# Separate tiles for the sums of weight blocks, and one place fewer for the partner blocks, in a Strassen gate and up projection

## The chip, the cores and the metric

One Trainium2 chip (trn2), one of its cores. The metric is the device time of one launch in microseconds; a kernel's time is the median of its runs. Engines are named as the profile names them: PE (TensorE's matmuls), PEld (its weight loads), DVE (VectorE), ACT (ScalarE), POOL (GpSimd) and SP (the queue that issues most transfers).

## The reference, cut to what matters

One layer of a decoder is computed for 1024 prompt rows and 32 sample rows: a mixer of convolution and attention, then a feed-forward part, then a last norm. The change lies in the feed-forward part alone:

```python
h2 = _rmsnorm(x, norm2_g) * (1 + sc2) + sh2
ffn = (jax.nn.silu(h2 @ w_gate) * (h2 @ w_up)) @ w_down
x = x + ga2 * ffn
```

All of it is in float32, with 1024 features, 2816 hidden features and 1056 rows.

## The kernel before, in words

Activations lie transposed: features on the 128 partitions, rows along the free dimension. A float32 product is made of three matmuls in a reduced format: the operand is split into a high part (`wh`, `xh`: a rounded copy by ACT) and a low part (`wl`, `xl`: operand minus high part, by DVE), and high x high, high x low and low x high are summed in PSUM.

The 1056 rows are cut into two **lanes** of 528, and each lane into halves of 264. For gate and for up, `block_product` (line 1357) makes, by a Strassen scheme of seven block products instead of eight, two blocks of 128 output columns at once: block f and its partner f + 11. `combos` (line 1234) makes the seven split operands of a lane; `weight_units` (line 1318) yields the seven split weight operands. A call of `block_product` is called a **product** here: seven **steps** (the loop at line 1389), each of four k-blocks with three matmuls per lane (lines 1396 to 1398). There are 24 products: gate and up of f = 0 for lane 0 alone, while lane 1 is still being normalised (line 1444); gate and up of f = 1 to 10 for both lanes; and between f = 4 and 5 the two of f = 0 for lane 1 (line 1451). Steps add into three PSUM banks; in between a partial product is held by ACT (`hold`, line 1379), and results go to the tile sg by DVE (`put`, line 1363). POOL then stores sg in a_d (line 1435).

For each product `weight_units` loads two raw tiles on the SP queue: r1 with the 1024 x 128 weights of block f (line 125, in the pool wp, tag raw, three places, which the high part of w_out's tiles used before and the loads of activations for the down projection use after, line 1487) and r2 with those of its partner f + 11 (line 1323, in a pool of its own, w3, three places). With a11 and a12 the halves of r1 and a21 and a22 those of r2, the weight operands of the seven steps are a11, a12, s2, s1, s3, s4, a22, where

```python
s1 = a21 + a22   (line 1340, tile sw)      s3 = a11 - a21   (line 1341, over a21)
s2 = s1 - a11    (line 1342, over a11)     s4 = a12 - s2    (line 1343, over a12)
```

POOL makes the four sums, 128 x 512 elements each. Four splits are made per product: r1 as a whole (ACT at line 131, DVE at line 137, 1024 columns), then the pairs (s2, s1) and (s3, s4), then a22 (ACT at line 1332, which the profile counts under line 93, and DVE at line 1333, 512 columns each). Their tiles wh and wl have two places each, so a split can be made when the one two before it has been used up.

Since s2 and s4 are written over r1, they wait until DVE has split r1, and r1's place is free only when s2 and s4 have been split. r2's place is free when s3 and a22 have been.

The order of the instructions on each engine is not written out here: it is set when the program is built, by priority and by what is ready. The weight loads, sums and splits are traced at high priority. After each product up to two of the 24 copies of the caches, DRAM to DRAM, are put on the SP queue behind the last r2 load (line 1426).

Ahead of this stage stands the output projection (`out_product`, line 1183) with the squares and sums for norm2 (`norm2_square`, line 1202); norm2 of the second lane and its `combos` run on ACT and DVE beside the first two products (lines 1439 to 1445). Behind it comes the down projection: `load_a` (line 1481) loads activations from a_d into the places of r1 and splits them (lines 1491 and 1492), and `load_down` (line 1496) loads and splits w_down.

Of the kernel before, what the change touches and what calls it, by code (L numbers as in the profile page):

```python
# [10 lines left out]
F32 = mybir.dt.float32  # L11
# [7 lines left out]
P = 128  # L19
D = 1024  # L20
KT = 8
# [38 lines left out]
def hybrid_step(  # L60
# [9 lines left out]
    nc = tc.nc  # L70
# [13 lines left out]
    def nm(s):  # L84
        cnt[0] += 1
        return f"{s}_{cnt[0]}"
# [5 lines left out]
    def act(out, in_, func=AF.Copy, **kw):  # L92
        return nc.scalar.activation(out, in_, func, **kw)  # L93
# [28 lines left out]
    def load_raw(src, nk):  # L122
        raw = wp.tile([P, T], F32, tag="raw", bufs=3, name=nm("raw"))[:, :D].rearrange("p (k c) -> p k c", c=P)
        with in_order(last_w[1]):
            last_w[0] = nc.sync.dma_start(raw[:, :nk], src)
        return raw
# [7 lines left out]
    def split_raw(raw, nk):  # L134
        wh, wl = split_high(raw, nk)
        with in_order(pre_done[0]):
            nc.vector.tensor_sub(wl[:, :nk], raw[:, :nk], wh[:, :nk].bitcast(F32))  # L137
        return wh, wl
# [1144 lines left out]
    sw = tc.alloc_tile_pool(name="sw", bufs=1, side="right", reuse_waits="tile")  # L1283
# [14 lines left out]
    w3 = tc.alloc_tile_pool(name="w3", bufs=1, reuse_waits="tile")  # L1298
# [19 lines left out]
    def weight_units(w, f):  # L1318

        with tc.high_priority():  # L1320
            r1 = load_raw(w[:, :, P * f:P * f + P], KT)
            r2 = w3.tile([P, KT, P], F32, tag="raw", bufs=3, name=nm("raw"))
            last_w[0] = nc.sync.dma_start(r2, w[:, :, P * (f + FH):P * (f + FH) + P])
            s1 = sw.tile([P, 4, P], F32, tag="sw", bufs=2, name=nm("sw"))

        def pair(p, q):
            wh = wp.tile([P, KT, P], F32R, tag="wh", bufs=2, name=nm("wh"))
            wl = wp.tile([P, KT, P], F32R, tag="wl", bufs=2, name=nm("wl"))
            for i, x in enumerate((p, q)):
                if x is not None:  # L1330
                    h = wh[:, 4 * i:4 * i + 4]
                    act(h, x)
                    nc.vector.tensor_sub(wl[:, 4 * i:4 * i + 4], x, h.bitcast(F32))  # L1333
            return [(wh, wl, 0), (wh, wl, 4)]


        a11, a12, a21, a22 = r1[:, 0:4], r1[:, 4:8], r2[:, 0:4], r2[:, 4:8]
        with tc.high_priority():
            u = split_raw(r1, KT)
            nc.gpsimd.tensor_add(s1, a21, a22)  # L1340
            nc.gpsimd.tensor_sub(a21, a11, a21)
            nc.gpsimd.tensor_sub(a11, s1, a11)
            nc.gpsimd.tensor_sub(a12, a12, a11)
        s2, s3, s4 = a11, a21, a12
        yield (*u, 0)
        yield (*u, 4)
        with tc.high_priority():
            u = pair(s2, s1)
        yield from u
        with tc.high_priority():  # L1350
            u = pair(s3, s4)
        yield from u
        with tc.high_priority():
            u = pair(a22, None)
        yield u[0]

    def block_product(w, f, lanes, sgs, up, hook=None):

        units = weight_units(w, f)
        banks = [[ps("s") for _ in lanes], [ps("pt") for _ in lanes], [ps("mm") for _ in lanes]]  # L1360
        keep = {}
# [232 lines left out]
```

## Time and profile before

| | before |
|---|---|
| time, median of 3 runs | 1378.84 us (1377.95 to 1380.05) |
| the profiled execution's own time | 1376.94 us |
| its span, first to last instruction | 1375.2 us |
| mean granted clock of TensorE | 0.966 of full speed |
| PE busy | 1307.9 us, 95% of the span |
| PEld busy | 1206.0 us, 88% |
| DVE busy | 716.9 us, 52% |
| ACT busy | 499.6 us, 36% |
| POOL busy | 212.1 us, 15% |

All rows come from one profiled execution; times are counted from its first instruction. In a row of the timeline stand the start, the duration, the engine, the line of the kernel, the operation, what is written from what, the shapes and the count, and in brackets how long the engine had been idle and what ended that. A row of the waits names the engine and what it was about to do, and behind the arrow who released it; then the total, the number of times and the longest. In a row of the chain stand start, duration and the work that the end of the program was waiting for. PE is counted as busy from a matmul's start to its modelled end. A wait for several things is put down to the last of them.

### The profile page before, as it was taken

What the parts mean: (1) busy time and instruction counts of PE and PEld (TensorE: products, weight loads), DVE (VectorE), ACT (ScalarE), POOL (GpSimd) and SP (SyncE); (2) the same over time, 40 slices, a digit from 0 to 9 for tenths busy, and PEclk for the clock granted to TensorE, in tenths of its full rate; (3) what the DMA queues carried; (4) which work ended last, traced back from release to release, by engine and by line L of the source; (5) the groups of instructions that cost most, each with busy time, mean ns of one, the idle gap of its engine ahead of it and who ended that gap; (6) DMA issues with size and microseconds to landing.
All of it is one profiled execution on the core that took longest, in us unless ns stands there. A gap on an engine that the chain in (4) does not pass through costs nothing.

```text
span 1375.2 us, 23628 instructions
## 1 busy us (share of the span) xinstructions
PE 1307.9 (95%) x9488; PEld 1206.0 (88%) x9488; DVE 716.9 (52%) x1448; ACT 499.6 (36%) x1077; POOL 212.1 (15%) x235
## 2 busy tenths in 40 slices
PE   8999998999899999996999999999999599999996
PEld 7767686859588979995999999999999599999996
DVE  5732364137324968779554465554454435353465
ACT  5442515242423325636333344333344302020244
POOL 3700000000000001232323233332231000000000
PEclk9999999969899999998999999999999899999998
DMA  9957474337463965783436344332451534141343
GB/s 315 310 194 256 147 256 151 93 101 255 123 182 103 236 217 168 245 261 109 143 120 231 100 184 132 108 109 83 162 188 61 197 132 141 47 141 47 95 152 128
DMA packets 188093, 220.80 MB, mean 161 GB/s; under 512 B 12426, under 2 KB 159367, under 8 KB 187472
## 3 DMA queue, kind: packets, MB, share of 16 engines
q1 hardware_dynamic: 169550, 173.89, 39.5%
q0 software_dynamic: 11504, 41.96, 9.1%
q10 hardware_dynamic: 6930, 3.45, 1.0%
q8 instruction: 74, 1.21, 0.4%
q14 instruction: 35, 0.29, 0.1%
HBM read 182.11 MB, written 64.21 MB: 179 GB/s over the span
## 4 chain that ended last, share of the span: by engine, by line
PE 73%; DVE 9%; issue 8%; DMA 7%; POOL 2%; ACT 1%; SPq 1%; DVEq 0%; POOLq 0%; ACTq 0%
PE pss L1398 6%; PE pss L1397 6%; PE pss L1396 6%; PE psmm L162 4%; PE psmm L163 4%; PE psmm L164 4%; PE pss L1509 3%; PE pss L1510 3%; PE pss L1511 3%; PE psmm L1509 3%; PE psmm L1510 3%; PE psmm L1511 3%; PE psmm L1397 3%; PE psmm L1396 3%; PE psmm L1398 3%
## 5 line engine op out<-in xcount | busy, mean ns | idle before, releaser
L93 ACT ACTIVATE wh<-raw 128x512 fp32r<-128x512 f32 (+2 forms) x200 | 152.7, 775 | 440.4 <-PE psmm L163 91.2
L1396 PE MATMUL pss<-xh,wh 128*128 128x264 f32 x704 | 201.1, 286 | 12.8 <-ACT wh L93 9.6
L1398 PE MATMUL pss<-xh,wl 128*128 128x264 f32 x704 | 201.2, 286 | 3.7 <-DVE wl L1333 3.4
L1397 PE MATMUL pss<-xl,wh 128*128 128x264 f32 x704 | 200.8, 285 | 0.0
L162 PE MATMUL psmm<-hh,wh 128*128 128x384 f32 (+1 forms) x528 | 176.9, 335 | 0.0
L163 PE MATMUL psmm<-hl,wh 128*128 128x384 f32 (+1 forms) x528 | 175.8, 333 | 0.0
L164 PE MATMUL psmm<-hh,wl 128*128 128x384 f32 (+1 forms) x528 | 174.7, 331 | 0.0
L137 DVE TENSOR_TENSOR wl<-raw,wh 128x1024 fp32r<-128x1024 f32 (+2 forms) x103 | 107.3, 1043 | 97.8 <-ACT wh L93 54.1
L1333 DVE TENSOR_TENSOR wl<-raw,wh 128x512 fp32r<-128x512 f32 x96 | 89.2, 940 | 118.3 <-ACT wh L93 117.0
L1396 PEld LDWEIGHTS pss<-xh,wh 128*128 128x128 f32 x704 | 133.4, 190 | 13.7 <-ACT wh L93 9.8
L1398 PEld LDWEIGHTS pss<-xh,wl 128*128 128x128 f32 x704 | 132.9, 189 | 5.0 <-DVE wl L1333 4.4
L1397 PEld LDWEIGHTS pss<-xl,wh 128*128 128x128 f32 x704 | 133.4, 189 | 0.0
L162 PEld LDWEIGHTS psmm<-hh,wh 128*128 128x128 f32 x528 | 100.8, 191 | 14.7 <-issue 11.5
L163 PEld LDWEIGHTS psmm<-hl,wh 128*128 128x128 f32 x528 | 100.9, 191 | 5.3 <-issue 4.9
L164 PEld LDWEIGHTS psmm<-hh,wl 128*128 128x128 f32 x528 | 101.4, 192 | 3.1 <-issue 2.8
L1396 PE MATMUL psmm<-xh,wh 128*128 128x264 f32 x352 | 101.0, 287 | 0.3 <-ACT wh L93 0.2
L1397 PE MATMUL psmm<-xl,wh 128*128 128x264 f32 x352 | 100.6, 286 | 0.0
L1398 PE MATMUL psmm<-xh,wl 128*128 128x264 f32 x352 | 100.1, 285 | 0.0
L1509 PE MATMUL pss<-ah,wh 128*128 128x384 f32 (+1 forms) x264 | 86.2, 326 | 14.7 <-ACT wh L93 14.7
L1510 PE MATMUL pss<-al,wh 128*128 128x384 f32 (+1 forms) x264 | 85.8, 325 | 0.0
L1511 PE MATMUL pss<-ah,wl 128*128 128x384 f32 (+1 forms) x264 | 85.7, 325 | 0.0
L1509 PE MATMUL psmm<-ah,wh 128*128 128x384 f32 (+1 forms) x264 | 85.4, 324 | 0.0
(324 smaller groups left out, 2896.8 us busy)
## 6 DMA issues: line engine op xcount, KB each, us to landing
ring<-in_w_ada_dram SPq DMA_DIRECT2D x32, 512.0 KB
out_dram<-in_cache_kv_dram SPq DMA_DIRECT2D x8, 2040.0 KB
raw<-in_w_in_dram SPq DMA_DIRECT2D x24, 512.0 KB
raw<-in_w_gate_dram SPq DMA_DIRECT2D x24, 512.0 KB
raw<-in_w_up_dram SPq DMA_DIRECT2D x24, 512.0 KB
a_d<-sg POOLq DMA_DIRECT2D x22, 528.0 KB, 3.3
a<-a_d SPq DMA_DIRECT2D x22, 528.0 KB
raw<-in_w_down_dram SPq DMA_DIRECT2D x48, 192.0 KB
```

The source lines that it names most:

```text
L93: return nc.scalar.activation(out, in_, func, **kw)
L137: nc.vector.tensor_sub(wl[:, :nk], raw[:, :nk], wh[:, :nk].bitcast(F32))
L162: nc.tensor.matmul(out, wh[:, k], h, start=(i == 0), stop=False)
L163: nc.tensor.matmul(out, wh[:, k], l, start=False, stop=False)
L164: last = nc.tensor.matmul(out, wl[:, k], h, start=False, stop=(i == n - 1))
L1333: nc.vector.tensor_sub(wl[:, 4 * i:4 * i + 4], x, h.bitcast(F32))
L1396: nc.tensor.matmul(o, wh[:, k0 + k], hi[:, k], start=st, stop=False, skip_group_check=True)
L1397: nc.tensor.matmul(o, wh[:, k0 + k], lo[:, k], start=False, stop=False, skip_group_check=True)
L1398: last = nc.tensor.matmul(o, wl[:, k0 + k], hi[:, k], start=False, stop=(k == 3), skip_group_check=True)
L1509: nc.tensor.matmul(o[:, :n], wh, ah[:, t0:t0 + n], start=(j == 0), stop=False)
L1510: nc.tensor.matmul(o[:, :n], wh, al[:, t0:t0 + n], start=False, stop=False)
L1511: nc.tensor.matmul(o[:, :n], wl, ah[:, t0:t0 + n], start=False, stop=(j == 2 * nf - 1))
```

## The change

s1, s2 and s4 get tiles of their own, from the pool sw, whose tag sw has four places instead of two; s3 is still written over a21. The pool w3, for r2, has two places instead of three. The order of the four sums in the text becomes s1, s2, s3, s4. Per partition the pool sw grows by 4 KB and w3 shrinks by 4 KB. Loads, splits, matmuls and the number of sums are the same.

```diff
         with tc.high_priority():
             r1 = load_raw(w[:, :, P * f:P * f + P], KT)
-            r2 = w3.tile([P, KT, P], F32, tag="raw", bufs=3, name=nm("raw"))
+            r2 = w3.tile([P, KT, P], F32, tag="raw", bufs=2, name=nm("raw"))
             last_w[0] = nc.sync.dma_start(r2, w[:, :, P * (f + FH):P * (f + FH) + P])
-            s1 = sw.tile([P, 4, P], F32, tag="sw", bufs=2, name=nm("sw"))
+            s1, s2, s4 = [sw.tile([P, 4, P], F32, tag="sw", bufs=4, name=nm("sw")) for _ in range(3)]
...
             u = split_raw(r1, KT)
             nc.gpsimd.tensor_add(s1, a21, a22)
+            nc.gpsimd.tensor_sub(s2, s1, a11)
             nc.gpsimd.tensor_sub(a21, a11, a21)
-            nc.gpsimd.tensor_sub(a11, s1, a11)
-            nc.gpsimd.tensor_sub(a12, a12, a11)
-        s2, s3, s4 = a11, a21, a12
+            nc.gpsimd.tensor_sub(s4, a12, s2)
+        s3 = a21
```

## Rows read from the trace of the kernel before

**Rows 1.** Busy time by stretch: us, PE, PEld, DVE, ACT, POOL (instructions), PEclk, DMA share, GB/s

```profile
600.00:620.00 20.00, 17.30 (x137) 16.74 (x136) 13.52 (x19) 9.17 (x18) 11.44 (x10) 1.00 0.96 321
620.00:640.00 20.00, 9.35 (x52) 8.62 (x51) 19.86 (x23) 15.80 (x27) 3.85 (x3) 0.74 0.42 157
...
660.00:1082.00 422.00, 421.26 (x3461) 420.26 (x3460) 212.33 (x335) 163.41 (x338) 120.94 (x102) 1.00 0.39 133
1082.00:1098.00 16.00, 1.33 (x8) 1.12 (x7) 8.38 (x8) 4.09 (x4) 1.93 (x3) 0.65 0.93 319
```

**Rows 2.** What PE waited for, 560 to 1110 us: total us, times, longest

```profile
PE pss L1509 <- ACT wh L93: 14.7, 1, 14.7
PE pss L1396 <- ACT wh L93: 9.6, 1, 9.6
...
PE pss L1396 <- ACT p L93: 2.3, 1, 2.3
```

**Rows 3.** What POOL waited for, whole execution

```profile
POOL raw L1342 <- DVE wl L137: 244.8, 23, 17.8
```

**Rows 4.** The chain of waits, 595 to 612 us: start, duration, what

```profile
596.28 1.25 SPq L1323
...
597.69 7.09 DMA raw<-in_w_gate_dram
...
605.98 1.35 DVE wl L137
...
607.82 1.00 DVE x L1147
...
608.90 0.43 ACT sq L93
...
609.35 1.06 DVE acx L1212
610.41 0.42 DVE x L1141
```

**Rows 5.** Timeline of SP: an r2 load, and the third load of activations

```profile
721.98 0.57 SPq L1323 DMA_DIRECT2D raw<-in_w_up_dram  x1
...
1070.37 0.32 SPq L1487 DMA_DIRECT2D a<-a_d  x1
```

**Rows 6.** Timeline of PE, output projection and the last product's first low-part matmul

```profile
596.93 0.28 PE L164 MATMUL psmm<-mh,wl 128*128 128x256 f32 x1
...
608.63 0.28 PE L164 MATMUL psmm<-mh,wl 128*128 128x256 f32 x1
...
1062.37 0.28 PE L1398 MATMUL pss<-xh,wl 128*128 128x264 f32 x1
```

**Rows 7.** Timeline of POOL: three of its sums

```profile
608.83 1.30 POOL L1343 TENSOR_TENSOR raw<-raw 128x512 f32<-128x512 f32 x1
...
728.39 1.29 POOL L1340 TENSOR_TENSOR sw<-raw 128x512 f32<-128x512 f32 x1 [12.80 <-DMA raw<-in_w_up_dram]
...
855.84 1.30 POOL L1341 TENSOR_TENSOR raw<-raw,raw 128x512 f32<-128x512 f32 x1
```

**Rows 8.** Timeline of DVE: adds for norm2, splits of weights, splits of activations

```profile
613.07 0.18 DVE L1147 TENSOR_TENSOR x<-x,gs 128x32 f32<-128x32 f32 x1
...
613.80 0.43 DVE L1212 TENSOR_TENSOR acx<-acx,sq 128x256 f32<-128x256 f32 x1
...
856.40 1.82 DVE L137 TENSOR_TENSOR wl<-raw,wh 128x1024 fp32r<-128x1024 f32 x1 [0.59 <-ACT wh L93]
...
1060.43 1.23 DVE L137 TENSOR_TENSOR wl<-raw,wh 128x1024 fp32r<-128x1024 f32 x1 [0.58 <-ACT wh L93]
...
1074.54 0.69 DVE L1333 TENSOR_TENSOR wl<-raw,wh 128x512 fp32r<-128x512 f32 x1 [4.20 <-ACT wh L93]
...
1083.06 3.59 DVE L1492 TENSOR_TENSOR al<-a,ah 128x1056 fp32r<-128x1056 f32 x3
```

**Rows 9.** DMA issues: what, KB each, median us from issue to landing

```profile
a_d<-sg POOLq DMA_DIRECT2D x22, 528.0 KB, 3.3
```

## The prediction

> **What bounds the kernel now.** I read the busy time by stage first [rows 1]. From 660 to 1082 us TensorE is busy 421.26 of 422 us: there the products of gate and up follow each other without a gap, and nothing that readies weights earlier can gain. The gaps are at both ends of that stretch: 2.70 and 10.65 us of idle TensorE in the two slices from 600 to 640 us, at a granted clock down to 0.74, and 14.67 us of the 16 from 1082 to 1098 us. The list of TensorE's waits says what ended them [rows 2]: 9.6 us for a split on ScalarE and 2.3 us for a held partial product at the start, and 14.7 us for the first split of w_down at the end. The wait that the change is aimed at is long, 244.8 us of POOL waiting for VectorE's split of r1 [rows 3]; but TensorE does not see it after 660 us, since weights are split a unit or two ahead. So the case is decided at the start, at the end, and by what is newly put in the way between.
>
> The chain of waits shows the start [rows 4]: the SP queue issues the third r2 load (1.25 us), then r1 of the first product, which takes 7.09 us to land; then ScalarE and VectorE split it (1.35 us on VectorE), and the last squares of norm2 follow behind on VectorE. From there the chain stays on VectorE's queue until the first product on both lanes.
>
> **The change, part by part.** The profiled execution took 1376.94 us at a span of 1375.2; its time is 1.9 us under the median of 1378.84, and I make the sum against 1376.94 and add the 1.9 at the end.
>
> *Third r2 place gone.* At 596 us three r2 loads go out ahead of the first r1. After, only two can. The issue itself saves little: r1's place is held by w_out's high part, whose last use is the matmul at 596.93 [rows 6], so r1 goes out at about 597.3 instead of 597.69: 0.4 us. The transfer saves more: 512 KB at the 321 GB/s of that slice [rows 1] are 1.6 us that no longer lie ahead of r1. Together 2.0 us on the chain. The bounds: 0, if r1's landing is set by other traffic in that slice, and 3.0, a quarter of the 7.09 us for one of four equal loads (1.8) and the whole issue of 1.25.
>
> *Sums no longer wait for the split.* s2 = s1 - a11 and s4 wrote over r1, so they waited for VectorE's split; now they need only r1 landed. In the first product they ran from 607.5 to 610.1 us, the fourth sum from 608.83 [rows 7], and under them VectorE's add for x took 1.00 us and its add of squares 1.06, where the same two take 0.18 and 0.43 without POOL [rows 4, 8]: 1.4 us on the chain. After, all four sums follow r1's landing and end before these adds, but run beside the split of r1 instead. A like split took 1.82 beside a sum and 1.23 without [rows 8], so I charge 0.6 back: 0.8 us gained (bounds 0 and 1.4).
>
> The start so gains 2.0 + 0.8 = 2.8 us. It is capped by what is late next: the last matmul of the output projection ends at about 608.9 us [rows 6], and its add, square and sum of squares (0.42 + 0.43 + 0.43 [rows 4, 8], and 0.18 for the samples) could be done at 610.4, where now they are at 614.2: 3.8 at most. The 9.6 us wait for the split of the second product stays: that split stands behind norm2 and the Strassen sums of lane 1 in ScalarE's order, and I take the order as it is.
>
> *Steady products.* The sums move off the path of ScalarE's second split. Cover: TensorE is never late there, so nothing is gained but part of the 0.74 us that 421.26 leaves of 422 [rows 1]; I take 0.2. POOL carries the same 96 sums. What is queued behind them on POOL are the stores of sg, whose tile has four places, one pair of products more than is in use; a store late by one wait of at most 17.8 us costs nothing.
>
> *Two r2 places.* Each r2 load waits for the split of a22 two products back instead of three. In the last product that split ended at 1075.2, 13.1 us after the product's first matmuls at 1062.1 [rows 6, 8]. What a load takes to land has two bounds: 1.6 us, its bytes at 321 GB/s, and 6.4, from the issue at 721.98 to the sum at 728.39 that waited for it, with another load beside it [rows 5, 7]; nearest is the 3.3 us of a store of 528 KB [rows 9]. Even at 6.4 r2 is there 19.5 us into a product of about 20.4 (1062.1 to where TensorE falls idle in the slice from 1082 [rows 1]), a whole product ahead of its use. Loads of r1 behind it on SP are two or three products ahead of theirs. Cost 0, unless POOL's sum then meets something (below).
>
> *Four places for sums, three used per product.* s2 of a product waits for the split of s1 of the one before, some 3 to 4 us into that product, 17 us ahead of need: 0.
>
> *r1 free earlier.* r1 is now free after its split and the sums, about 1061.7 us in the last product instead of after the split of s4. The third load of activations for the down projection, which went out at 1070.37 [rows 5], can go 8.7 us earlier. But VectorE's subtractions for all three loads stand in its order behind the last product's results, at 1083.06 [rows 8], and the next loads wait for these. With the order as it is the gain is 0.
>
> Sum: 2.8 + 0.2 = 3.0 us. 1376.94 - 3.0 = 1373.9 us, against the median 1375.8 us, 0.2% faster. About 0.2% (2.8 us) is what a measurement of this kernel can tell from no change, so the forecast lies on that edge.
>
> **Rivals.**
>
> *Slower: the sum lands on the split.* In a steady product POOL's first sum, which had its source early, now starts when r2 lands. With r2 issued at 13.1 us and landed 3.3 to 6.4 us later, POOL works from 16.4 to 19.5 us on, for one or two sums of 1.3 us each. VectorE splits r1 of the next product 1.7 us before that begins (1060.43 against 1062.1), so at 18.7, and the first use is at 1062.37, only 0.7 us after its end [rows 6, 8]. The row at 856.40 shows the meeting: a sum from 855.84 to 857.14, an overlap of 0.74 us, and 0.59 us more on the split [rows 7, 8]. A meeting over a whole sum costs about 1.3 us less the 0.7 of slack, 0.6 us; two sums, 1.9. It decides once the landing takes over 5 us, or over 3.7 if two sums run on end. At 0.6 us in each of some 18 products that is 11 us: 1389.8, or with meetings in half of them 1384. Against it: at the nearest landing, 3.3 us, the first sum is over at 17.7, before the split. The Trainium skill, SBUF — State Buffer, "Who interferes with whom", says that a VectorE instruction with two SBUF inputs and a POOL one that reads SBUF exclude each other for a whole instruction, whichever starts first. The row at 856.40 is near to that, with 0.59 of 0.74; by the rule in full the split would wait 0.74 and the price per meeting hardly changes. Chance 0.2.
>
> *No change: VectorE eats it.* VectorE is busy 19.86 of the 20 us from 620 to 640 us [rows 1], and a start that is 3 us earlier can be spent there when the sums of the next products fall elsewhere. Gain under 1.5 us: 1377.3 to 1379.5. For it speaks that full queue; against it, that the chain runs through the very load that goes away. Chance 0.25.
>
> *Much faster: the order changes.* The engines' orders are set when the program is built, by what is ready. If the second product's split comes earlier on ScalarE, part of the 9.6 us goes; if the activations' subtractions come among the last results, up to 8.7 of the 14.7 us goes. Between 5 and 14 us: 1365 to 1374. For it: both splits ran long after their data had landed. Against: POOL's waits had no part in either order that the trace shows. Chance 0.15.
>
> **How the numbers follow.** The forecast has 0.4; its own range is 1374 to 1377.3, where the next rival begins. Six tenths of it lie past 0.2%. Faster: 0.24 + 0.15 and some of the edge, 0.42. Slower: 0.2 and a little for orders that turn out worse, 0.23. The same: 0.35. The range leaves out the far half of either outer rival: 1367 to 1383.
>
> **What would show it.** Right: POOL's wait for the split of r1 (244.8 us) is gone; the first r1 lands near 603 us; the wait of 2.3 us shrinks; the wait of 9.6 stays, some 3 us earlier; the end keeps its 14.7. Wrong: waits of TensorE between 680 and 1060 us on the split of r1, with VectorE's splits of 1024 columns at a mean well over 1.23 us; or another order on ScalarE between 619 and 634 us, or on VectorE after 1076.

## The result, and the profile after

The changed kernel is slower: 1386.26 us median of 20 runs (1374.92 to 1391.63 without one disturbed run) against 1377.45 us of the kernel before, a ratio of 1.0055 with a 95% interval of 1.0034 to 1.0076. That is 7.6 us, where 3.0 us of gain were forecast.

The profiled execution took 1376.12 us (span 1374.3), no longer than the one of before. The first thing to read is why. Windows of the kernel after: stretch, then busy time of PE, PEld, DVE, ACT and POOL with their instructions, granted clock, DMA share and GB/s.

```profile
200.00:400.00 200.00, 188.64 (x1243) 154.36 (x1242) 81.61 (x219) 70.76 (x180) 8.30 (x17) 0.96 0.52 163
600.00:620.00 20.00, 12.12 (x72) 11.27 (x73) 14.90 (x13) 9.34 (x19) 10.01 (x8) 0.74 0.68 238
620.00:640.00 20.00, 18.10 (x146) 17.57 (x145) 19.86 (x29) 16.46 (x30) 5.26 (x2) 1.00 0.58 192
640.00:660.00 20.00, 15.47 (x95) 14.43 (x94) 18.35 (x15) 8.19 (x16) 13.50 (x8) 0.74 0.14 46
760.00:860.00 100.00, 94.22 (x753) 92.95 (x752) 57.62 (x78) 38.81 (x78) 40.60 (x31) 0.98 0.44 154
860.00:960.00 100.00, 100.00 (x826) 100.00 (x825) 51.92 (x84) 36.55 (x75) 30.01 (x25) 1.00 0.29 97
1080.00:1100.00 20.00, 4.53 (x25) 4.14 (x24) 9.83 (x11) 4.93 (x5) 1.95 (x3) 0.68 0.80 260
```

The stretch from 200 to 400 us lies far ahead of anything that the diff touches. Its granted clock was 0.96 here; the same window of the kernel before has 0.89:

```profile
200.00:400.00 200.00, 187.88 (x1158) 150.81 (x1156) 80.08 (x216) 66.65 (x172) 8.25 (x17) 0.89 0.49 152
```

TensorE got 85 matmuls further in it. So the output projection's last matmul ended at 598.78 us instead of 608.91 [rows 6], and the execution began the changed stage with a head start of 10.1 us. In all 18 profiles of this study that end lies either at 599 to 602 us, with a clock of 0.94 to 0.96 in that window, or at 606 to 612, with 0.87 to 0.90, whatever the kernel. I therefore compare the **stage time**, from that end to the end of the last product: 473.8 us before, 483.2 after, 9.4 us more. The end behind it kept its wait (15.5 us against 14.7 [rows 2]), and from the last product to the end of the program it takes as long as before (292.4 us against 292.5). So this pair of executions differs by 9.4 us in the stage alone, where the medians lie 8.8 us apart.

Inside the stage, 640 to 660 and 760 to 860 us have new gaps; the second stretch was all but full before [rows 1]. TensorE's waits from 660 to 1085 us, after (there were 0.7 us in all before):

```profile
PE pss L1398 <- DVE wl L1333: 4.3, 2, 4.1
PE psmm L1398 <- DVE wl L1333: 1.0, 1, 1.0
PE pss L1398 <- DVE wl L137: 0.9, 3, 0.5
```

One wait is most of it. Here is what surrounds it, DVE, POOL and PE in the timeline after:

```profile
766.54 0.68 POOL L1435 DMA_DIRECT2D a_d<-sg  x1 [28.14 <-DVE sg L1370]
767.13 1.41 POOL L1340 TENSOR_TENSOR sw<-raw 128x512 f32<-128x512 f32 x1
768.36 0.83 POOL L1435 DMA_DIRECT2D a_d<-sg  x1
768.96 1.54 POOL L1341 TENSOR_TENSOR sw<-sw,raw 128x512 f32<-128x512 f32 x1
...
772.68 1.51 POOL L1340 TENSOR_TENSOR sw<-raw 128x512 f32<-128x512 f32 x1
769.24 5.51 DVE L1333 TENSOR_TENSOR wl<-sw,wh 128x512 fp32r<-128x512 f32 x1 [2.19 <-ACT wh L93]
775.02 1.68 DVE L1333 TENSOR_TENSOR wl<-sw,wh 128x512 fp32r<-128x512 f32 x1
776.75 0.59 PE L1398 MATMUL pss<-xh,wl 128*128 128x264 f32 x1 [4.09 <-DVE wl L1333]
```

The sums of pair 4's gate product stand on POOL **behind the stores of sg**, which waited 28.14 us for the product before to be finished. So they start when their splits are due. VectorE's split of s1 begins at 769.24 and takes 5.51 us, where such a split alone takes 0.68: it ends at 774.75, as POOL's unbroken run from 768.96 to 774.19 is over. What TensorE waits for is the split behind it, that of s2 at 775.02, which itself takes 1.68 beside the next sums. The wait is 4.09 us, and then TensorE runs a while at a lower granted clock, after:

```profile
770.00:775.00 5.00, 2.66 (x22) 2.45 (x21) 5.00 (x2) 0.63 (x1) 4.31 (x5) 1.00 0.34 122
775.00:780.00 5.00, 3.25 (x15) 3.25 (x16) 5.00 (x5) 2.27 (x5) 4.53 (x3) 0.66 0.25 74
780.00:785.00 5.00, 5.00 (x43) 5.00 (x43) 0.45 (x2) 1.69 (x4) 0.00 (x0) 1.00 0.02 3
```

15 matmuls fill 3.25 us of a stretch whose mean clock is 0.66, between the levels of 1.2 and 2.4 GHz, where 43 fill 5 us at 1.00.

The start shows the same picture (SP, ACT, POOL, DVE, PE after):

```profile
586.13 1.22 SPq L1427 DMA_DIRECT2D out_dram<-in_cache_kv_dram  x1
587.52 0.45 SPq L125 DMA_DIRECT2D raw<-in_w_gate_dram  x1
599.68 0.42 ACT L93 ACTIVATE sq<-x 128x256 f32<-128x256 f32 x1 [2.67 <-DVE x L1147]
600.20 1.06 ACT L93 ACTIVATE wh<-raw 128x1024 fp32r<-128x1024 f32 x1
599.88 0.87 POOL L1214 DMA_DIRECT2D xT_d<-x  x1 [2.21 <-DVE x L1147]
600.69 1.37 POOL L1341 TENSOR_TENSOR sw<-sw,raw 128x512 f32<-128x512 f32 x1
...
605.78 1.37 POOL L1342 TENSOR_TENSOR raw<-raw,raw 128x512 f32<-128x512 f32 x1
600.13 5.86 DVE L1212 TENSOR_TENSOR acx<-acx,sq 128x256 f32<-128x256 f32 x1 [0.54 <-ACT sq L93]
605.92 2.31 DVE L137 TENSOR_TENSOR wl<-raw,wh 128x1024 fp32r<-128x1024 f32 x1
608.28 0.59 PE L1398 MATMUL pss<-xh,wl 128*128 128x264 f32 x1 [4.40 <-DVE wl L137]
```

Five sums run behind a store of x (to `xT_d`, line 1214). The add of squares, 0.43 us alone [rows 8], is held for 5.86, and TensorE waits 4.40 us for the split behind it. In turn the 9.6 us wait of [rows 2] is gone: ACT makes the second product's split at 620.66 and not at 633.32, the first row after and the second before:

```profile
620.66 1.05 ACT L93 ACTIVATE wh<-raw 128x1024 fp32r<-128x1024 f32 x1
633.32 1.04 ACT L93 ACTIVATE wh<-raw 128x1024 fp32r<-128x1024 f32 x1
```

The third place is the one-lane products of pair 0, after pair 4 (DVE, SP, POOL, PE after):

```profile
804.98 0.69 DVE L1333 TENSOR_TENSOR wl<-raw,wh 128x512 fp32r<-128x512 f32 x1 [1.94 <-ACT wh L93]
811.21 1.23 DVE L137 TENSOR_TENSOR wl<-raw,wh 128x1024 fp32r<-128x1024 f32 x1
812.50 0.37 SPq L125 DMA_DIRECT2D raw<-in_w_up_dram  x1
812.91 0.58 SPq L1323 DMA_DIRECT2D raw<-in_w_up_dram  x1
820.45 1.29 POOL L1340 TENSOR_TENSOR sw<-raw 128x512 f32<-128x512 f32 x1 [5.88 <-DMA raw<-in_w_up_dram]
828.78 0.39 PE L1398 MATMUL psmm<-xh,wl 128*128 128x264 f32 x1 [1.01 <-DVE wl L1333]
```

Here POOL does wait for the load: r2 goes out at 812.91, and the first sum starts 7.5 us later, in products of some 10 us. Its place had been free since 805.67, when the split of a22 two products back (804.98) was done. But on SP's queue r2 stands behind the load of r1 for two products further on (812.50), and that one goes out as VectorE's split of the r1 whose place it takes ends (811.21 to 812.44).

### The profile page after: what moved, and what is told of

It reads as the page before. It is cut to its first block, busy times and chain, and to the rows that moved or that the text cites. A ratio compares the mean times of both kernels' runs of the same rounds, so it can differ in the third digit from the quotient of the medians.

```text
span 1374.3 us, 23672 instructions
## 1 busy us (share of the span) xinstructions
PE 1302.3 (95%) x9488; PEld 1204.5 (88%) x9488; DVE 728.2 (53%) x1448; ACT 499.5 (36%) x1077; POOL 226.5 (16%) x235
## 4 chain that ended last, share of the span: by engine, by line
PE 72%; issue 9%; DVE 8%; DMA 6%; ACT 2%; POOL 1%; SPq 1%; DVEq 0%; POOLq 0%; ACTq 0%
PE pss L1398 5%; PE pss L1396 5%; PE pss L1397 5%; PE psmm L162 4%; PE psmm L163 4%; PE psmm L164 4%; PE pss L1509 3%; PE pss L1510 3%; PE pss L1511 3%; PE psmm L1509 3%; PE psmm L1510 3%; PE psmm L1511 3%; DMA qb<-qs_d 3%; PE psmm L1397 3%; PE psmm L1396 3%
## 5 line engine op out<-in xcount | busy, mean ns | idle before, releaser
L93 ACT ACTIVATE wh<-raw 128x512 fp32r<-128x512 f32 (+2 forms) x152 | 124.9, 822 | 386.7 <-PE psmm L163 90.5
L137 DVE TENSOR_TENSOR wl<-raw,wh 128x1024 fp32r<-128x1024 f32 (+2 forms) x103 | 110.3, 1072 | 92.2 <-ACT wh L93 49.7
L1398 PEld LDWEIGHTS pss<-xh,wl 128*128 128x128 f32 x704 | 134.3, 191 | 14.7 <-DVE wl L137 8.6
L1509 PE MATMUL pss<-ah,wh 128*128 128x384 f32 (+1 forms) x264 | 86.2, 326 | 15.5 <-ACT wh L93 15.5
L1510 PE MATMUL psmm<-al,wh 128*128 128x384 f32 (+1 forms) x264 | 85.4, 324 | 0.0
```

The source lines that it names most:

```text
L1398: last = nc.tensor.matmul(o, wl[:, k0 + k], hi[:, k], start=False, stop=(k == 3), skip_group_check=True)
L1509: nc.tensor.matmul(o[:, :n], wh, ah[:, t0:t0 + n], start=(j == 0), stop=False)
L1510: nc.tensor.matmul(o[:, :n], wh, al[:, t0:t0 + n], start=False, stop=False)
```

## The experiments

Below is what each profile lost against the kernel before. I took the starts of the matmuls of gate and up, counted from the end of the output projection, and read at which time the same share of them was reached. "Start" is up to 98 us into the stage, "pair 4" 98 to 191, "one-lane" 191 to 240, "rest" from there to the last product. The ratio is of the timed runs to those of the kernel before taken beside them, with its 95% interval. The kernel before itself loses 1.9 us in the one-lane window, as the two rows show in which these products are moved away; what stands in that column is on top of this.

| kernel | start | pair 4 | one-lane | rest | stage, us | ratio |
|---|---|---|---|---|---|---|
| before | 0 | 0 | 0 | 0 | 473.8 | 1 |
| changed | 2.0 | 5.8 | 1.2 | 0.4 | 483.2 | 1.0055 (1.0034 to 1.0076) |
| changed, again | 1.5 | 5.7 | 3.7 | 0.2 | 484.9 | 1.0069 (1.0035 to 1.0102) |
| changed, s2 waits | 0.9 | 5.6 | 6.5 | -0.1 | 486.6 | 1.0086 (1.0047 to 1.0124) |
| before, two r2 places | 3.0 | 5.2 | 4.6 | 1.3 | 487.9 | 1.0062 (1.0032 to 1.0092) |
| changed, fills for sums | -13.5 | 0 | 3.5 | -0.2 | 463.6 | 0.9896 (0.9854 to 0.9939) |
| changed, sg stores on ACT | 1.1 | 0 | 3.8 | 0.3 | 478.9 | 1.0050 (1.0026 to 1.0075) |
| own tile for s2, three r2 places | -2.5 | 0 | 0.3 | -0.2 | 471.4 | 0.9989 (0.9964 to 1.0013) |
| changed, sums on VectorE | -8.1 | 0 | 2.8 | -0.2 | 468.3 | 0.9961 (0.9930 to 0.9993) |
| changed, one-lane pair after pair 7 | 1.3 | 6.5 | -1.9 | 4.4 | 484.1 | 1.0094 (1.0052 to 1.0136) |
| before, one-lane pair after pair 7 | -0.6 | 0 | -1.9 | 5.7 | 477.0 | 1.0030 (0.9995 to 1.0066) |
| two r2 places, sg stores on ACT | 1.7 | 0 | 5.6 | -0.1 | 481.0 | 1.0083 (1.0048 to 1.0117) |
| before, sums on VectorE | -7.3 | 0 | -1.2 | -0.2 | 465.1 | 0.9938 (0.9906 to 0.9970) |
| before, first sum five times | 14.9 | 1.2 | 4.5 | 8.3 | 502.6 | 1.0225 (1.0147 to 1.0302) |
| before, first sum twice and fills | 5.8 | 0 | 1.5 | 4.1 | 485.1 | 1.0096 (1.0057 to 1.0134) |
| changed, all stores on ACT | -2.4 | 0.9 | 3.7 | 0.2 | 476.2 | 1.0055 (1.0019 to 1.0090) |
| before, all stores on ACT | -5.0 | 0 | 1.5 | -0.2 | 470.1 | 1.0027 (0.9991 to 1.0063) |

**The changed kernel again.**

> The changed kernel once more, for a second profiled execution and a second interval. Every theory expects about 1.005 of the kernel before. Theory T (POOL's sums, no longer held by the split of r1, run on end and hold VectorE's splits): TensorE idle 660 to 1060 us again at several us instead of 0.7, with the waits on VectorE's low parts, and more of them if this execution is longer than 1376 us.

The same waits come back (4.40 and 4.09 us), in an execution of 1390.85 us whose output projection ended at 610.91. Of the 14.7 us between this execution and the first, 12.1 are thus the head start described above, and the loss is there in both. That a longer execution would have more of these waits did not come true; only the one-lane products lost more (3.7 us against 1.2).

**s2 waits for the split of r1 again.**

> The changed kernel, with s2 made to wait for VectorE's split of r1 again; tiles and places stay as changed. Theory T: POOL's bursts are paced again, TensorE's idle from 660 to 1060 us falls under 2 us, the ratio to the kernel before is 0.998 to 1.002. Rival (the lost r2 place): nothing changes, 1.004 to 1.007, and TensorE's waits in the steady stretch stay. Rival (order of the start): the steady waits may shrink, but 600 to 660 us keeps its 14 us of idle TensorE and the ratio stays over 1.003.

```
- nc.gpsimd.tensor_sub(s2, s1, a11)
+ i2 = nc.gpsimd.tensor_sub(s2, s1, a11)
+ tc.add_manual_dep(i2.ins, last_split[0].ins.name, ...)
```

A miss for the theory of that moment: 1.0086, and the wait at pair 4 is still 3.83 us. That the sums lost the wait of [rows 3] is not the cause.

**Only the lost place.**

> The kernel before with two places for r2 instead of three, all else as before. Theory T: the place alone costs little, 0.999 to 1.002, and TensorE's idle from 660 to 1060 us stays near 0.7 us. Rival (the lost r2 place is the cause): 1.004 to 1.007, with TensorE's waits on VectorE's low parts in the steady stretch.

```
- r2 = w3.tile(..., tag="raw", bufs=3)
+ r2 = w3.tile(..., tag="raw", bufs=2)
```

The rival won: one place fewer, with nothing else of the change, loses as much as the change and more (14.1 us of the stage against 9.4 and 11.1). POOL, VectorE and PE with two places:

```profile
769.85 0.68 POOL L1435 DMA_DIRECT2D a_d<-sg  x1 [18.18 <-DVE sg L1370]
776.02 1.48 POOL L1342 TENSOR_TENSOR raw<-sw,raw 128x512 f32<-128x512 f32 x1
772.55 5.50 DVE L1333 TENSOR_TENSOR wl<-sw,wh 128x512 fp32r<-128x512 f32 x1 [2.19 <-ACT wh L93]
779.43 0.59 PE L1396 MATMUL pss<-xh,wh 128*128 128x264 f32 x1 [3.57 <-ACT wh L93]
833.18 0.39 PE L1398 MATMUL psmm<-xh,wl 128*128 128x264 f32 x1 [2.84 <-DVE wl L1333]
```

It works through the order: in the kernel before the first sums of that product stand ahead of the stores, here behind them. POOL before:

```profile
757.62 1.29 POOL L1340 TENSOR_TENSOR sw<-raw 128x512 f32<-128x512 f32 x1 [1.23 <-DVE wl L1333]
775.31 0.68 POOL L1435 DMA_DIRECT2D a_d<-sg  x1
```

The hold is not all of the wait here: the sum s2 is over only at 777.50, some 1.7 us after TensorE ran out of work, and ACT's split of it, which TensorE waited for, could not come before that. At the one-lane products r2's place is free at 808.42, and r2 goes out at 821.71, again right behind a load of r1 (821.30).

**Fills in place of the sums.**

> The changed kernel without the four sums of weight blocks: POOL fills their tiles with a constant instead, four writes of the same size per product that read nothing from SBUF, so the weights of four of the seven steps are not the reference's. Theory T: the splits on VectorE beside POOL are no longer stretched, the mean of those of 1024 columns falls to about 1.1 us and TensorE's idle from 660 to 1060 us under 1.5 us; ratio 0.992 to 0.999. Rival (late r2 landing or the start's order): the waits stay at several us and the ratio over 1.002.

```
- nc.gpsimd.tensor_add(s1, a21, a22)
+ nc.gpsimd.memset(s1, 0.5)
```

(and so for the other three sums). Pair 4 is clean and the start gains 13.5 us, more than expected (0.9896). The splits of 512 columns fall to a mean of 0.69 us, those of 1024 to 1.23 and not 1.1. From 660 to 1060 us TensorE is idle for 2.9 us and not 1.5: the one-lane loss stays. But a fill takes 0.53 us and mostly waits for no load, so this run takes lateness away together with the reads.

**The stores on another queue.**

> The changed kernel with the stores of sg issued by SP instead of POOL. Stage time is counted here and below from the end of the output projection's last matmul to the end of the last product: 473.8 us before, 483.2 and 484.9 in two executions of the changed kernel. Theory T2 (with two r2 places the sums come to stand behind the stores of sg on POOL, are let go only when a product is over, and then run on end beside the splits that are due): no steady wait of TensorE of 4 us near 176 us into the stage, steady idle under 2 us, stage 474 to 479. Rival (the load of r2 itself lands too late): the waits stay, stage 483 or more. On SP the stores may hold the loads behind them; then waits on the split of r1 show up, and the test is spoilt.

> The changed kernel with the stores of sg issued by ACT instead of POOL. Theory T2: as with SP, no steady wait of 4 us, stage 474 to 479, unless ACT's own splits stand behind a store, which would show as waits of TensorE on ACT's high parts. Rival (late r2 landing): steady waits on VectorE's low parts stay, stage 483 or more.

```
- nc.gpsimd.dma_start(a_d[...], sg)
+ nc.sync.dma_start(a_d[...], sg)
```

(in the second run nc.scalar).
On SP the test was spoilt, as feared: 15 waits on the split of r1, 17.3 us in all, and three more of 35.5 us in all, the longest 15.62, for results on VectorE; the stage takes 541.8 us, a ratio of 1.037. On ACT the wait at pair 4 is gone, as expected, with two r2 places still. The end pays 2.0 us for the stores on ACT (17.5 us against 15.5).

**Half the change, three places.**

> Half of the change: s2 has a tile of its own (s1 and s2 share the two places of sw, s4 is written over a12), and r2 keeps its three places. Theory T2 (the lost place is the trigger): stage within 3 us of 473.8, steady idle under 2 us, ratio 0.996 to 1.002. Rival (unpaced sums are enough, whatever the places): stage 480 or more and steady waits on VectorE's low parts, ratio 1.003 to 1.008.

```
- s1, s2, s4 = [sw.tile(..., bufs=4) for _ in range(3)]
- nc.gpsimd.tensor_sub(s4, a12, s2)
+ s1, s2 = [sw.tile(..., bufs=2) for _ in range(2)]
+ nc.gpsimd.tensor_sub(a12, a12, s2)
```

(against the changed kernel; r2 has bufs=3 again). Stage 471.4 us. With the places kept, s2 in a tile of its own costs nothing, and gains nothing that could be measured (0.9989, 0.9964 to 1.0013). All tiles of the change beside three r2 places were not tried.

**The sums on VectorE.**

> The changed kernel with the four sums on VectorE, so that nothing of them stands behind a store on POOL and nothing runs beside the splits; VectorE gets 96 operations more. Theory T2: no split of 512 columns of over 2 us, steady idle under 2 us, stage 468 to 478, at the start bounded by VectorE's fuller queue. Rival (late r2 landing): the steady waits of 4 us stay, since the sums still need r2; stage 483 or more.

> The kernel before, with its three places for r2, and with the four sums on VectorE instead of POOL. The changed kernel with the sums on VectorE took 468.3 us for the stage and still lost 2.9 us at the one-lane products. Theory T2: here that loss is gone and the gain at the start (8 us less than before) stays: stage 464 to 468, ratio 0.990 to 0.996, faster than both kernels. Rival (VectorE fills up): the start gives back what the splits gain, ratio 0.998 or more.

```
- nc.gpsimd.tensor_add(s1, a21, a22)
+ nc.vector.tensor_add(s1, a21, a22)
```

(and the other three sums; first in the changed kernel, then in the one before). The stages, 468.3 and 465.1 us, are as expected; but in the first TensorE is idle for 3.0 us from 660 to 1060 us, where I expected under 2, most of it a wait of 2.4 us at the one-lane products. With three places and the sums on VectorE the kernel is the fastest of the study that makes all sums, 1368.98 us. Windows of that kernel:

```profile
600.00:620.00 20.00, 19.48 (x157) 19.13 (x156) 13.36 (x30) 8.51 (x18) 1.75 (x2) 1.00 1.06 349
640.00:660.00 20.00, 19.78 (x161) 19.39 (x160) 16.87 (x27) 10.78 (x21) 0.67 (x1) 1.00 0.32 98
660.00:1060.00 400.00, 399.83 (x3291) 399.44 (x3290) 224.46 (x400) 157.70 (x324) 13.13 (x19) 1.00 0.39 136
```

VectorE has 96 operations more and room for them, and the start takes 7.3 us less than before. The two runs differ by the change alone: with no sum on POOL it still costs 3.2 us, 4.0 at the one-lane products less 0.8 at the start.

**Moving the one-lane products.**

> The changed kernel with the two one-lane products of pair 0 placed after pair 7 instead of after pair 4, nothing else. So far the changed kernel loses its time at three places: 1 to 2 us at the start, 5.4 us at the gate product of pair 4 (some 178 us into the stage) and 1.2 to 4 us in the one-lane products behind it (some 220 us in). Theory T2 (a product of half the length has half the time to bring r2 in, and two places look only two products ahead): the wait near 220 us goes, and 1 to 4 us are lost some 345 us into the stage instead; the wait of 4.1 us is tied to the same order of loads and moves to the gate product of pair 7, some 300 us in, or goes. Rival (the losses belong to the place in time, to traffic or to what the engines carry over from the start): they stay at 178 and 220 us.

> The kernel before with the same move of the two one-lane products, as the pair to the run on the changed kernel. Theory T2: three places suffice for the short products wherever they stand, stage 472 to 476 us, ratio 0.998 to 1.002, idle of TensorE under 1.5 us in the steady stretch. Rival (the short products alone decide): 2 us and more lost at 345 us into the stage.

```
- if f == 4:
+ if f == 7:
      ffn_pair(0, [1], w2, 4)
```

Half right. The late loss moved with the short products: counting the 1.9 us that the kernel before loses there, from 3.1 or 5.6 us behind pair 4 to 4.4 us behind pair 7. The wait of 4.1 us did not: it is tied to pair 4's order, not to them. And the kernel before lost 5.7 us behind pair 7 with three places, 3.8 more than the 1.9 behind pair 4, which I had not expected. Timeline of that run:

```profile
938.16 0.67 POOL L1435 DMA_DIRECT2D a_d<-sg  x1
938.76 1.39 POOL L1340 TENSOR_TENSOR sw<-raw 128x512 f32<-128x512 f32 x1
938.91 4.24 DVE L1333 TENSOR_TENSOR wl<-raw,wh 128x512 fp32r<-128x512 f32 x1 [0.92 <-ACT wh L93]
943.21 0.59 PE L1398 MATMUL pss<-xh,wl 128*128 128x264 f32 x1 [2.54 <-DVE wl L1333]
```

Three sums stand behind a store, and hold a split for 4.24 us until they are over. Three places are no protection by themselves; the kernel before merely had an order without such a run in its steady stretch.

**Both conditions at once.**

> The kernel before with two places for r2 and with the stores of sg issued by ACT instead of POOL. With two places alone the stage took 487.9 us, 5.3 us of it lost at the gate product of pair 4. Theory T2: that loss needs the sums to stand behind the stores and goes; the 1 to 5 us at the one-lane products stay, since there the load itself is late; stage 478 to 484. Rival (the late load is the whole cause): both losses stay, stage 486 or more.

As expected: without stores of sg on POOL the lost place costs nothing at pair 4, and 5.6 us at the short products.

**Lateness or reads?**

> The kernel before with the first sum of each product made five times over on POOL: some 6.5 us on end that read SBUF, the result as it was. Theory T2 (a run of POOL's reads holds a VectorE operation with two SBUF inputs until it is over): splits of 512 and 1024 columns of 4 to 7 us appear in the steady stretch, their means there rise over 1.5 us and TensorE loses 15 to 80 us against the kernel before. Rival (only the lateness of the sums counts): the splits keep their means of 0.7 to 0.9 and 1.25 us, and what is lost is the same as in the run beside this one.

> The kernel before with the first sum made twice and seven fills of its tile between the two, each of 0.53 us by the fills seen in the run without sums: some 6.3 us of POOL that mostly write and do not read SBUF, the result as it was. Theory T2: no split over 2.5 us, means near those of the kernel before, and at least three times less lost than in the run beside this one. Rival (lateness alone): as much is lost as there.

```
+ for _ in range(5):
      nc.gpsimd.tensor_add(s1, a21, a22)
```

(in the second run the sum, seven fills of s1, and the sum).
About the same length of POOL work costs 28.9 us when it reads SBUF and 11.4 when it mostly fills: 2.5 times, where I asked for 3. Splits from 660 to 1060 us, first with reads, then with fills (count | busy, mean ns | idle before):

```profile
L1333 DVE TENSOR_TENSOR wl<-raw,wh 128x512 fp32r<-128x512 f32 x80 | 103.1, 1302 | 89.0 <-ACT wh L93 88.1
```

```profile
L1333 DVE TENSOR_TENSOR wl<-raw,wh 128x512 fp32r<-128x512 f32 x81 | 76.8, 958 | 109.4 <-ACT wh L93 108.1
```

In the kernel before these splits take 908 ns in the mean. Means of over 1.5 us did not come, and only one split of over 3 us (6.34): most splits take turns with the sums. So a run of sums alone does not hold a split; something more is needed. In the profiles with the sums on POOL there are 24 VectorE operations of over 3 us for one instruction between 570 us and the end of the stage, and each began within 1.2 us after the start of a store's issue on POOL, with at least two sums right behind it (in some cases with a second store between them). Their length follows the number of these sums: 3.0 to 4.2 us with two, 4.2 with three, 5.5 to 5.9 with four, 6.3 with five; with one, no operation took more than 2.3. It is a pattern and not a law: in the kernel before, an add of squares began at 613.80 [rows 8], 0.25 us after such a start, with three sums behind, and took 0.43; so did the same add in one other run. The Trainium skill, SBUF — State Buffer, "Who interferes with whom", says that a VectorE instruction with two SBUF inputs contends with a GpSimd one that reads SBUF and not with one that only writes. The run with fills alone agrees: its splits keep 0.69 us in the mean.

**No store on POOL.**

> The changed kernel with the stores of sg and those of xT_d issued by ACT instead of POOL; the sums stay on POOL. Theory T3 (a VectorE operation with two sources in SBUF that begins during a store's issue on POOL is held until the sums behind it leave a gap; without a store they alternate): no such operation of over 2.6 us for one instruction from 570 to 1100 us; the add of squares that took 5.86 us at the start takes under 2.3, and the wait of 4.4 us of TensorE there goes; the loss at the one-lane products stays. Stage 470 to 478 us; the end gains nothing, since ACT carries the stores (17.5 us there with sg's alone). Rival (runs of four sums hold without a store too): the 5.86 and the 4.4 us stay, stage 479 or more.

> The kernel before with the stores of sg and of xT_d issued by ACT. Before, one split took 4.19 us at the start, behind a store of xT_d. Theory T3: no such operation of over 2.6 us; stage 468 to 474 us against 473.8, where the wait of 9.6 us for ACT may move with ACT's order. Rival: the 4.19 us stays and the stage is the same.

```
- nc.gpsimd.dma_start(xT_d[...], ...)
+ nc.scalar.dma_start(xT_d[...], ...)
```

(and the same for sg). Right in both: no VectorE operation of over 2.4 us, the 5.86 us add (now 1.51) and the 4.4 us wait are gone, and the stages are 476.2 and 470.1 us. Against the kernel before as it was, what remains of the change's loss is the 3.7 us of the one-lane products and 0.9 at pair 4. Against the kernel before with the same stores, the change still costs 6.1 us: 2.6 at the start, 0.9 at pair 4, 2.2 at the one-lane products and 0.4 behind. So the hold is not the whole cause; where the 2.6 us at the start come from was not taken apart. As kernels they gain nothing: the end takes 21.5 and 24.3 us, in which TensorE waits for ACT's split of w_down; ACT now has the last stores of sg in its queue.

## Why the prediction was wrong

**The step that failed is "Two r2 places ... Cost 0".** Three things were wrong in it. I let each r2 load go out as its place comes free, 13.1 us into the last product, a two-lane one of 20.4 us, and wrote of the loads of r1 only as standing behind it. At the one-lane products, of about 10 us, r2 stood behind a load of r1 and went out 7.2 us after its place was free; there it is late (7.5 us from issue to first sum), for 1.2 to 6.5 us. My own row at 721.98 [rows 5] is such a load: a load of r1 went out at 721.56, and the place had been free since 706.08. I asked what stands behind the sums on POOL and named the stores, but not whether the sums might come to stand behind the stores; with two places they do, and that is 5 to 6 us at pair 4. And I wrote "I take the order as it is", while the order is made anew from what is ready when, and a place fewer changes that.

**The start** was forecast at 2.8 us of gain and lost 1.5 to 2.0; with the lost place alone it lost 3.0. *Third r2 place gone*, 2.0 us, gave nothing: a copy of the caches took its slot, and r1 went out 11.3 us ahead of the output projection's end (587.52 against 598.78), as before (597.69 against 608.91, 11.2). It was not the bound any more either: its split stood behind the last square of norm2 on ACT. *Sums no longer wait for the split*, 0.8 us, had its sign turned: the sums did not follow r1's landing but stood on POOL behind the stores of x, and the hold of 5.86 us came of it. The 9.6 us wait, which I let stay, went, as the rival *Much faster* had it for the order; but new waits ate the gain, 2.5 us for ACT before the first matmul, the 4.4 for VectorE and 4.6 from 640 to 660 us among them: up to 664 us TensorE waits 15.5 us in all, where it waited 16.0.

**Right** were the wait of 244.8 us, which is gone and worth nothing that could be measured; and the end, 15.5 us for 14.7, so that "r1 free earlier" brought 0. "Four places for sums" at 0 was not tested by itself.

The rival "the sum lands on the split" had the right sign and the right pair of engines, but the wrong meeting and price: not 0.6 us on the split of r1 in half the products, but one hold of 5.5 us on the split of s1, which costs 5.8 us with the lower clock behind it. That its 1384 to 1389.8 us enclose the measured 1386.26 is luck. The 1.8 and 1.2 us rows [rows 8] from which I priced it are the common case, and the rare one is what TensorE sees.

That the lost place is the trigger is shown by one run that takes only the place and one that keeps it; that the pair-4 wait needs the stores of sg on POOL by two runs without them. That r2 is late at the one-lane products because of the load of r1 ahead of it is read from the traces; no run changed that order alone. Why the order comes out that way at pair 4 and not elsewhere was not tested.

## What to carry to other kernels

Before giving up a buffer place, find the shortest consumer in the loop, not the typical one, and time the load against that, from when its queue lets it go and not from when its place is free. On an engine that also issues stores, look at what the elementwise work stands behind: a store that waits for a finished result makes everything after it late (here one waited 28.14 us). Where another engine has room, as VectorE had here at 52%, moving the sums there can pay (0.6% here) where more tiles for them did not.

## What the hardware showed that was not expected

A VectorE operation with both sources in SBUF is usually slowed to taking turns with POOL's sums (0.69 us to 1.3 in the mean, with five first sums on end). But one that begins around a store's issue on POOL, with two or more sums queued right behind, is as a rule held until that run has a gap: 5.86 us for 0.43, 5.51 for 0.68, 4.24 for 0.69, 6.34 in the longest case. It is there 24 times in 12 profiles, and not once in the two in which POOL issued no store of this stage while the sums stayed there, nor in the one with fills between the sums. Why the store matters is not shown.
